# Expert stage of a hybrid S5 / attention / MoE layer: token lists from a DRAM table, padded bias rows, longer lo parts, paired PSUM banks

## Chip, cores and metric

One core of one Trainium2 chip runs the whole layer in one launch. The metric is the device time of a run in microseconds (us); lower is better.

## The reference

The layer normalises 1024 tokens of 1024 channels (with 256 context tokens beside them), mixes them by a state-space branch and a windowed attention, and then sends each token to 4 of 32 experts. The change touches only that last part:

```python
logits = (xf @ w_router + b_router)
top_v, top_i = lax.top_k(logits, 4)
gates = jax.nn.softmax(top_v, axis=-1)
...
gu = xb @ w_gate_up[e] + b_gate_up[e]
glu, lin = jnp.split(gu, 2, axis=-1)
glu = jnp.minimum(glu, 7.0)
lin = jnp.clip(lin, -7.0, 7.0)
act = glu * jax.nn.sigmoid(1.702 * glu) * (lin + 1)
return act @ w_down[e] + b_down[e]
...
y = zeros.at[row_tok].add(y_rows * row_gate[:, None])
```

All of it is float32. Each expert has a gate-and-up matrix of 1024 x 2048 and a down matrix of 1024 x 1024, 12 MB together.

## The kernel before

**Stages.** Some 1080 us of projections, state-space scan, attention and router come first; then the 32 experts run one after the other (about 1090 to 2670 us); a last stage normalises and stores. The change is in the expert stage and in the small preparations just ahead of it.

**Precision.** A float32 product is made of three TensorE products. A weight tile is split into a high part `wh`, written by ScalarE (ACT, line 1491), and a low part `wl = raw - wh`, by VectorE (DVE, line 1493). Both are computed in `Weights.prepare` for a piece of 1 MB, in two halves of 1024 columns, with a half's `wl` right behind its `wh`. Raw pieces come by 512 KB transfers on SyncE's queue, up to 8 halves ahead; `wh` and `wl` have four buffers each.

**Experts.** `ORDER` takes the experts by rank of their number of tokens, one from the top and one from the bottom in turn: 15 *wide* ones of two blocks (128 + 128 down to 128 + 32 rows) and 17 *narrow* ones of one block of 128. I call the place in that order the position, from 0; even positions up to 28 are wide. Every expert has 12 steps: 0 to 7 the up product (`up`/`act` when narrow, `up_wide`/`act_wide` when wide), 8 to 11 the down product (`down`). In each step the program emits, for TensorE (PE), ACT and DVE in an order written by hand: the part of the elementwise work that is due (`after`), the split of the weights of a later step (`prepare`), a turn of the next expert's rows in steps 1, 6, 7 and 10 (`x_parts`: four transposes on TensorE, line 1277, into a bank `tp`, a high copy on ACT, a subtraction on DVE, line 1286), and then the step's matmuls (`main`). In steps 5 and 9 of a narrow expert the activations are turned as well (`TURN`, line 1277 with `tp<-ident,t`).

**Lists.** Which tokens an expert gets is found by one-hot matrices: `places` makes `oh` (8 DVE instructions, line 1197), and `slots` multiplies `info` by it (8 matmuls of 6 columns per block, each with its weight load, line 1213, tile `sl`), sums and decodes on DVE (lines 1217 to 1226) and gives row indices `ri`, destinations `wi` and gates `gt`. This is done two positions ahead. Then GpSimd (POOL) gathers the rows (`x<-xm_d`, line 1255) and, after the expert, adds results to `acc_d` with an indirect DMA (line 1442). GpSimd executes its queue in order.

**Bias.** A wide expert adds its bias on ACT. A narrow one adds it with a matmul at line 1320: `sel` (64 rows, one of them set by `pick`) times `bgu` (64 rows), once per pair of up steps, 4 times an expert.

**PSUM.** Five banks `mm` rotate among products, two `tp` among turns, one `lg` is for `sl`.

Of the kernel before, what the change touches and what calls it, by code (L numbers as in the profile page):

```python
# [19 lines left out]
D = 1024  # L20
# [61 lines left out]
def body(tc, a, o):  # L82
# [3 lines left out]
    with es:  # L86
# [20 lines left out]
        K.tabe_d = dram.tile([64, 1], I32, name="tabe_d")  # L107
        K.cst = cst
# [973 lines left out]
def rank_consts(tc, a, K, tmp):  # L1082
    nc = tc.nc
    v = nc.vector
    late = K.late
    K.g2 = late.tile([128, D], F32, name="g2")
# [15 lines left out]
    K.pick = late.tile([64, 32], F32, name="pick")  # L1102
# [39 lines left out]
def ranks(tc, a, K):  # L1142
# [30 lines left out]
    v.tensor_copy(K.pick, K.pk.bitcast(F32))  # L1173
# [27 lines left out]
def slots(tc, K, pool, ps, o, info, blocks, steps=((0, 6),)):  # L1201
# [5 lines left out]
    p = ps.tile([128, 512], F32, tag="lg", name="sl")  # L1207
    out = [(pool.tile([128, 1], I32, tag="ri%d" % b, name="ri"), pool.tile([128, 1], I32, tag="wi%d" % b, name="wi"),
            pool.tile([128, 1], F32, tag="gt%d" % b, name="gt")) for b in range(len(blocks))]
    for c0, c1 in steps:  # L1210
# [16 lines left out]
        yield out  # L1227

# [4 lines left out]
class Expert:  # L1233
# [76 lines left out]

    def up(self, c, w):

        nc, K = self.nc, self.K
        if c % 2 == 0:
            self.gu = K.mm.tile([128, 512], F32, tag="mm", name="up")
# [16 lines left out]
    def act(self, q):  # L1332
# [3 lines left out]
        x = self.whole(self.gu, nb, ("hg", "hu")[q])[0:nb]  # L1336
        t = P.tmp.tile([128, 512], F32, tag=("sg", "um")[q], name="t")[0:nb]
# [10 lines left out]
    def up_wide(self, c, w):  # L1348
# [5 lines left out]
        self.uw = []  # L1354
        for i in range(2):
            p = K.mm.tile([128, 512], F32, tag="mm", name="uw")
# [4 lines left out]
            self.uw.append(p[:, 0:2 * n].rearrange("p (q n) -> p q n", q=2))  # L1361

    def act_wide(self, c):
# [4 lines left out]
        t = [P.tmp.tile([128, 512], F32, tag=("sg", "um")[q], name="t") for _ in range(2)]  # L1368
        x, y = [a[:, 0:n] for a in t], [a[:, 256:256 + n] for a in t]
        for i in range(2):  # L1370
            nc.scalar.activation(out=y[i], in_=self.uw[i][:, 1], func=ACTF.Identity, bias=self.bias[:, q * 8 + j0 + i:q * 8 + j0 + i + 1])  # L1371
        for i in range(2):
            v.tensor_tensor(x[i], self.uw[i][:, 0], y[i], ALU.add)
        if q == 0:
            yield
            for i in range(2):
                nc.scalar.activation(out=y[i], in_=x[i], func=ACTF.Sigmoid, scale=SWIGLU)
            yield
            for i in range(2):
                v.tensor_tensor(x[i], x[i], y[i], ALU.mult)  # L1380
            self.g = x
            return
        for i in range(2):
            v.tensor_scalar(x[i], x[i], LIMIT + 1, 1 - LIMIT, ALU.min, ALU.max)
        for i in range(2):
            v.scalar_tensor_tensor(x[i], self.g[i], TOP, x[i], ALU.min, ALU.mult)
        yield
        for i in range(2):
            nc.scalar.activation(out=self.a[:, j0 + i, 0:n], in_=x[i], func=ACTF.Copy)
        yield  # L1390
        for i in range(2):
# [30 lines left out]
    def down(self, c, k0, w):  # L1422
        if k0 == 0:
            if c == 0:
                self.y = []
            self.y.append([self.K.mm.tile([128, 512], F32, tag="mm", name="dn")[0:nb if nb > 64 else 2 * nb] for nb in self.blocks])
# [24 lines left out]
class Weights:  # L1451
# [8 lines left out]
    def add(self, eid, wide=False):  # L1460
        for m, kn, k, c in WIDE if wide else CHUNKS:
            self.todo += [(eid, m, kn // 2, k + i * kn // 2, c) for i in range(2)]

    def fetch(self):
# [5 lines left out]
        n = 1024 // kn  # L1470
# [3 lines left out]
        nc.sync.dma_start(out=r, in_=w[:, k:k + kn])  # L1474
        self.raw.append(r)

    def prepare(self):
# [6 lines left out]
        kn, n = self.raw[0].shape[1:3]  # L1484
        hi = P.ws.tile([128, 2 * kn, n], F32R, tag="wh", name="wh")
        lo = P.ws.tile([128, 2 * kn, n], F32R, tag="wl", name="wl")
        self.ready.append((hi, lo))
        for i in range(2):
# [17 lines left out]
def expert_pools(tc, a, K, es, deep):  # L1506
    P = Ctx()
    pool = lambda name, bufs=1, **k: es.enter_context(tc.tile_pool(name=name, bufs=bufs, **k))
    P.ahead = 8 if deep else 4
# [5 lines left out]
    P.tmp = pool("etmp", 2)  # L1515
# [69 lines left out]
def expert_consts(tc, a, K, late):  # L1585
    nc = tc.nc
    K.bgu = late.tile([64, 2 * D], F32R, name="bgu")
    K.full = late.tile([64, 256], F32, name="full")
    nc.gpsimd.memset(K.full, 1.0)
    nc.gpsimd.memset(K.full[:, 192:256], 0.0)  # L1590
    br = K.wp.tile([128, KT, 256], F32, tag="raw", name="br").rearrange("p k n -> p (k n)")[0:64]
    for j in range(2):
        nc.sync.dma_start(out=br[j * 32:(j + 1) * 32], in_=a["b_gate_up"])
    nc.gpsimd.tensor_scalar(br[:, D:], br[:, D:], 1.0, 1.0, ALU.add, ALU.mult)
# [6 lines left out]
def moe(tc, a, K):  # L1601
    nc = tc.nc
    es = ExitStack()
    with es:
        pool = lambda st, name, bufs=1, **k: st.enter_context(tc.tile_pool(name=name, bufs=bufs, **k))
        K.mm = pool(es, "emm", 5, space=PSUM)
        K.tp = pool(es, "etp", 2, space=PSUM)
        K.lg = pool(es, "elg", 1, space=PSUM)
        with ExitStack() as st:
# [7 lines left out]
            def expert_id(nc, K, r):  # L1617
                if r not in regs:
                    regs[r] = nc.sync.value_load((eid if P.ahead == 8 else K.eid)[0:1, r:r + 1], min_val=0, max_val=31)
                return regs[r]  # L1620

            def place(i):
                if i < len(ORDER):
                    r = ORDER[i]
                    return places(tc, K, P.li, lambda t: K.posr[:, t, r:r + 1], CAPS[r])

            def lists(i, o, *steps):
                if i < len(ORDER):
                    r = ORDER[i]
                    return slots(tc, K, P.li, K.lg, o, lambda t: K.info[:, t, r, :], BLOCKS[CAPS[r]], *steps)  # L1630
# [9 lines left out]
            P.ahead = 2  # L1640
            with tc.manual_schedule(engines={mybir.EngineType.PE, mybir.EngineType.DVE, mybir.EngineType.Activation}):
# [7 lines left out]
                P.ahead = 8  # L1649
# [8 lines left out]
            prev = None  # L1658
            with tc.manual_schedule(engines={mybir.EngineType.PE, mybir.EngineType.DVE, mybir.EngineType.Activation}):
                for i in range(len(ORDER)):  # L1660
                    xs = iter(nxt.x_parts()) if nxt else iter(())
                    for c in range(12):
# [4 lines left out]
                        weave(prev.store(1) if c == 0 and prev else None, cur.after(c), W.prepare(), x)  # L1667
# [54 lines left out]
def rest(tc, a, K):  # L1722
    nc = tc.nc
    v = nc.vector
    with ExitStack() as es:
# [4 lines left out]
        with tc.For_i(0, count, 1) as i:  # L1730
# [484 lines left out]
def host(inputs):  # L2215
# [16 lines left out]
    w["route"] = route_table()  # L2232
    w["sink"] = f("attn_sink")[0]
# [26 lines left out]
```

## Time and profile before

| what | value |
|---|---|
| median of 3 runs | 2745.44 us (2743.88 to 2748.95) |
| the profiled execution | 2748.94 us |
| its span in the profile | 2746.8 us |
| mean granted TensorE clock | 0.948 |
| PE / DVE / ACT / POOL busy, share of the span | 91% / 80% / 54% / 10% |
| moved by DMA | 662.57 MB, 241 GB/s in the mean |

The span is the time from the first instruction to the last; 2.1 us of the profiled execution lie around it. Busy shares are means over stages with different limits: in the first 1080 us several engines take turns, in the expert stage TensorE hardly stops. The chain of work that ended last holds only the closing normalisation, so it tells little of the expert stage.

### The profile page before, as it was taken

The page shows a single profiled execution, that of the slowest core. Times are in us where ns is not written, and L with a number is a line of the kernel's source. Part 1 is how long each engine was busy: PE and PEld are TensorE (multiplying, and loading weights), DVE is VectorE, ACT ScalarE, POOL GpSimd, SP SyncE. Part 2 cuts the span into 40 slices and gives each one's busy share as a digit, 9 for nine tenths or more (in the row PEclk, how much of TensorE's full clock was granted, in tenths as well). Part 3 has the DMA queues.
Part 4 walks back from the last instruction along what each step waited for, and adds up shares of the span by engine and source line. Part 5 has one row for each costly group of instructions (what it writes and reads, how often), then busy time and mean ns, then how long its engine had stood idle before and what let it go on. Part 6 is the DMA issues. An engine that isn't in the chain of part 4 may idle for free. (4 is left out here: it accounts for less than half of the span.)

```text
span 2746.8 us, 41465 instructions
## 1 busy us (share of the span) xinstructions
PE 2513.2 (91%) x14030; PEld 2113.3 (77%) x14030; DVE 2190.4 (80%) x4354; ACT 1471.6 (54%) x2394; POOL 273.7 (10%) x173
## 2 busy tenths in 40 slices
PE   6799999889989886899999999999999999999990
PEld 1598887767778775788878878888988887888770
DVE  9735797348787757787987987988989899989995
ACT  0622112657766312555665665666666666666661
POOL 3300000000000004010100100111011011101113
PEclk8799999999999876899999999999999999999995
DMA  7434623644686782797987987998998999899984
GB/s 250 163 121 145 209 92 114 181 160 156 229 303 242 278 294 97 238 287 218 299 266 239 306 271 243 308 300 252 301 305 269 288 310 306 274 298 303 311 279 146
DMA packets 400937, 662.57 MB, mean 241 GB/s; under 512 B 36976, under 2 KB 203760, under 8 KB 393616
## 3 DMA queue, kind: packets, MB, share of 16 engines
q1 hardware_dynamic: 388416, 615.83, 67.0%
q0 software_dynamic: 11872, 42.47, 6.7%
q8 instruction: 112, 1.84, 0.3%
q10 hardware_dynamic: 432, 1.57, 0.2%
q14 instruction: 105, 0.86, 0.1%
HBM read 570.63 MB, written 89.15 MB: 240 GB/s over the span
## 5 line engine op out<-in xcount | busy, mean ns | idle before, releaser
L1493 DVE TENSOR_TENSOR wl<-raw,wh 128x1024 fp32r<-128x1024 f32 x768 | 921.6, 1220 | 162.4 <-ACT wh L1491 161.4
L1491 ACT ACTIVATE wh<-raw 128x1024 fp32r<-128x1024 f32 x768 | 789.6, 1052 | 244.0 <-PE dn L1309 88.7
L1359 PE MATMUL uw<-x,wh 128*128 128x320 f32 (+5 forms) x1920 | 578.3, 365 | 0.2 <-issue 0.2
L1360 PE MATMUL uw<-x,wl 128*128 128x192 f32 (+4 forms) x1920 | 500.2, 261 | 0.0
L1359 PEld LDWEIGHTS uw<-x,wh 128*128 128x128 f32 x1920 | 363.1, 189 | 23.5 <-issue 0.3
L1360 PEld LDWEIGHTS uw<-x,wl 128*128 128x128 f32 x1920 | 368.2, 192 | 0.5
L1306 PE MATMUL dn<-wh,a 128*128 128x512 f32 (+4 forms) x752 | 298.7, 397 | 0.0
L1307 PE MATMUL dn<-wl,a 128*128 128x512 f32 (+4 forms) x752 | 293.5, 390 | 0.0
L1309 PE MATMUL dn<-wh,a 128*128 128x512 f32 (+3 forms) x608 | 238.5, 392 | 0.6 <-DVE a L1286 0.6
L1306 PE MATMUL up<-wh,x 128*128 128x512 f32 x544 | 221.8, 408 | 0.0
L1442 POOL DMA_INDIRECT acc_d<-y,wi x47 | 118.9, 2531 | 959.5 <-DVE y L1440 815.8
L1309 PE MATMUL up<-wh,x 128*128 128x512 f32 x544 | 213.0, 392 | 0.0
L1307 PE MATMUL up<-wl,x 128*128 128x512 f32 x544 | 212.3, 390 | 0.0
L1371 ACT ACTIVATE t<-uw,bias 128x160 f32<-128x160 f32 (+5 forms) x240 | 98.6, 419 | 131.8 <-PE uw L1360 130.9
L1306 PEld LDWEIGHTS dn<-wh,a 128*128 128x128 f32 (+4 forms) x752 | 135.7, 180 | 37.8 <-issue 4.1
L1307 PEld LDWEIGHTS dn<-wl,a 128*128 128x128 f32 (+4 forms) x752 | 135.8, 181 | 33.8
L1309 PEld LDWEIGHTS dn<-wh,a 128*128 128x128 f32 (+3 forms) x608 | 112.8, 186 | 28.4 <-DVE a L1286 2.7
L1306 PEld LDWEIGHTS up<-wh,x 128*128 128x128 f32 x544 | 102.3, 188 | 27.4 <-issue 8.4
L1309 PEld LDWEIGHTS up<-wh,x 128*128 128x128 f32 x544 | 102.1, 188 | 22.4
L1307 PEld LDWEIGHTS up<-wl,x 128*128 128x128 f32 x544 | 102.4, 188 | 18.8
L51 PE MATMUL mm<-whi,uh 128*128 128x256 f32 x320 | 108.4, 339 | 4.4 <-DVE r L307 4.4
L52 PE MATMUL mm<-wlo,uh 128*128 128x256 f32 x320 | 107.7, 337 | 0.0
(529 smaller groups left out, 4970.7 us busy)
## 6 DMA issues: line engine op xcount, KB each, us to landing
raw<-w_gate_up SPq DMA_DIRECT2D x512, 512.0 KB
raw<-w_down SPq DMA_DIRECT2D x256, 512.0 KB
mw<-w_mod SPq DMA_DIRECT2D x64, 256.0 KB
raw<-w_in SPq DMA_DIRECT2D x13, 1024.0 KB
whi<-wo SPq DMA_DIRECT2D x10, 1024.0 KB
wlo<-wo SPq DMA_DIRECT2D x10, 1024.0 KB
raw<-w_mod SPq DMA_DIRECT2D x8, 1024.0 KB
gate_d<-gs SPq DMA_DIRECT2D x16, 512.0 KB
```

Of the source, the lines that this page charges most:

```text
L51: nc.tensor.matmul(out, lhsT=lsel(lh, k), rhs=rsel(rh, k), start=start and k == 0, stop=False)
L52: nc.tensor.matmul(out, lhsT=lsel(lh, k), rhs=rsel(rl, k), start=False, stop=False)
L1306: nc.tensor.matmul(ps, lhsT=h, rhs=wh[:, k], start=st, stop=False)
L1307: nc.tensor.matmul(ps, lhsT=h, rhs=wl[:, k], start=False, stop=en and nb <= 64)
L1309: nc.tensor.matmul(ps, lhsT=X[:, k0 + k, lo:lo + nb], rhs=wh[:, k], start=False, stop=en)
L1359: nc.tensor.matmul(p[:, 0:2 * n], lhsT=wh[:, k, fs], rhs=self.x[:, k, 0:2 * n], start=k == 0, stop=False)
L1360: nc.tensor.matmul(p[:, 0:m], lhsT=wl[:, k, fs], rhs=self.x[:, k, 0:m], start=False, stop=k == KT - 1)
L1371: nc.scalar.activation(out=y[i], in_=self.uw[i][:, 1], func=ACTF.Identity, bias=self.bias[:, q * 8 + j0 + i:q * 8 + j0 + i + 1])
L1442: nc.gpsimd.indirect_dma_start(out=K.acc_d, out_offset=bass.IndirectOffsetOnAxis(ap=wi[0:nb], axis=0), in_=o[0:nb], in_offset=None, bounds ...
L1491: nc.scalar.activation(out=h, in_=r, func=ACTF.Copy)
L1493: nc.vector.tensor_tensor(l, r, h, ALU.subtract)
```

## The change

1. The lists of the experts at positions 6 to 31 are read from a table `list_d` in DRAM (32 x 1280 rows of 4 numbers), by small transfers on GpSimd's queue (`table`). The table is first filled with a default from an input (655 KB, on SyncE's queue), and then `spread` writes into it, two pieces of work per step in positions 0 to 2: DVE finds each token's four slots and gates, GpSimd scatters them in 32 indirect DMAs of 128 rows of 16 bytes. Positions 0 to 5 keep the one-hot way.
2. The bias matmul has 128 rows; the upper 64 rows of both operands are zeros.
3. The low part is one DVE instruction of 2048 columns, after both ACT halves of 1024; a raw tile is 1 MB, filled by two transfers.
4. A wide step has its two products in a pair of banks (`two`, two pairs), and ACT and DVE mostly work on both at once. Narrow steps have two single banks (`one`). `sl` uses a `tp` bank.
5. `rank_gates` keeps a second copy of the gates, made by ACT.

The core of the difference:

```diff
+    nc.sync.dma_start(out=K.list_d, in_=a["lists"])
...
-    p = ps.tile([128, 512], F32, tag="lg", name="sl")
+    p = ps.tile([128, 512], F32, tag="tp", name="sl")
...
+def spread(tc, K, pool):
+    nc = tc.nc
+    v = nc.vector
+    t_ = lambda n, w, d=F32: pool.tile([128] + w, d, bufs=1, name=n)
+    base, key, mx, oh = t_("lb", [32]), t_("lk", [8, 32]), t_("lx", [8, 8]), t_("lo", [4, 32])
+    idx, pay = t_("li", [8, 4], I32), t_("lp", [8, 4, 4], I32)
+    v.tensor_scalar(base, K.route[:, 0:32], float(LIST), None, ALU.mult)
+    v.memset(pay, 0)
+    yield
+    v.scalar_tensor_tensor(key, K.posr, 0.0, base.unsqueeze(1).to_broadcast([128, 8, 32]), ALU.is_gt, ALU.mult)
+    yield
+    v.tensor_tensor(key, key, K.posr, ALU.add)
+    yield
+    for t in range(8):
+        v.max(out=mx[:, t], in_=key[:, t])
+        v.tensor_scalar(pay[:, t, :, 0:2], K.route[:, 64:65].unsqueeze(2).to_broadcast([128, 4, 2]), 128.0 * t, None, ALU.add)
+        yield
+    v.tensor_scalar(idx, mx[:, :, 0:4], -1.0, None, ALU.add)
+    for t in range(8):
+        yield
+        v.tensor_tensor(oh, key[:, t].unsqueeze(1).to_broadcast([128, 4, 32]), mx[:, t, 0:4].unsqueeze(2).to_broadcast([128, 4, 32]), ALU.is_equal)
+        v.tensor_tensor(oh, oh, K.gr[:, t].unsqueeze(1).to_broadcast([128, 4, 32]), ALU.mult)
+        yield
+        v.reduce_sum(pay[:, t, :, 2].bitcast(F32), oh, axis=AX.X)
+        for j in range(4):
+            nc.gpsimd.indirect_dma_start(out=K.list_d, out_offset=bass.IndirectOffsetOnAxis(ap=idx[:, t, j:j + 1], axis=0),
+                                         in_=pay[:, t, j], in_offset=None, bounds_check=32 * LIST - 1, oob_is_err=True)
+            yield
...
-            s = P.pk.tile([64, 256], F32R, tag="pk", name="pk")
-            nc.vector.tensor_scalar(s, K.full, self.pick, None, ALU.mult)
-            self.sel = s[:, 0:128] if self.n == 128 else s[:, 128:256]
+            self.sel = P.pk.tile([128, 128], F32R, tag="pk", name="pk")
+            nc.vector.tensor_scalar(self.sel, K.full, self.pick, None, ALU.mult)
...
+    def banks(self, name):
+        return self.K.mm.tile([128, 2, 512], F32, tag="two", name=name)
...
-        for i in range(2):
-            v.tensor_tensor(x[i], self.uw[i][:, 0], y[i], ALU.add)
+            nc.scalar.activation(out=y[:, i], in_=uw[:, i, n:2 * n], func=ACTF.Identity, bias=self.bias[:, q * 8 + j0 + i:q * 8 + j0 + i + 1])
+        v.tensor_tensor(x, uw[:, :, 0:n], y, ALU.add)
...
-        for i in range(2):
-            ks = slice(i * kn, (i + 1) * kn)
-            h, l, r = (x.rearrange("p k n -> p (k n)") for x in (hi[:, ks], lo[:, ks], self.raw.pop(0)))
-            nc.scalar.activation(out=h, in_=r, func=ACTF.Copy)
-            h = h.bitcast(F32)
-            nc.vector.tensor_tensor(l, r, h, ALU.subtract)
-            yield
+        h, l, r = (x.rearrange("p k n -> p (k n)") for x in (hi, lo, raw))
+        for i in (0, 1024):
+            nc.scalar.activation(out=h[:, i:i + 1024], in_=r[:, i:i + 1024], func=ACTF.Copy)
+            if i == 0:
+                yield
+        nc.vector.tensor_tensor(l, r, h.bitcast(F32), ALU.subtract)
+        yield
...
-        K.mm = pool(es, "emm", 5, space=PSUM)
+        K.mm = pool(es, "emm", 2, space=PSUM)
         K.tp = pool(es, "etp", 2, space=PSUM)
-        K.lg = pool(es, "elg", 1, space=PSUM)
...
+            def table(r):
+                out = []
+                for b, nb in enumerate(BLOCKS[CAPS[r]]):
+                    x = P.li.tile([128, 4], I32, tag="tab%d" % b, name="tab")
+                    nc.gpsimd.dma_start(out=x[0:nb], in_=K.list_d[r * LIST + b * 128:r * LIST + b * 128 + nb])
+                    out.append((x[:, 0:1], x[:, 1:2], x[:, 2:3].bitcast(F32)))
+                yield out
...
-                        weave(prev.store(1) if c == 0 and prev else None, cur.after(c), W.prepare(), x)
+                        weave(prev.store(1) if c == 0 and prev else None, cur.after(c), W.prepare(), x, limit(to_lists, 2))
```

Two places show how instructions move. The first is GpSimd's queue at the start of the expert stage, from the last gather that is common to both (row form: line, operation, destination from sources, shape). Before:

```order
L1255 DMA x<-xm_d,ri 128x1024 x4
L1442 DMA acc_d<-y,wi 1152x1024 x2
L1255 DMA x<-xm_d,ri 128x1024
L1442 DMA acc_d<-y,wi 1152x1024
L1255 DMA x<-xm_d,ri 128x1024 x2
```

And in the change:

```order
L1294 DMA x<-xm_d,ri 128x1024 x4
L1264 DMA list_d<-lp,li 40960x4 x8
L1477 DMA acc_d<-y,wi 1152x1024
L1264 DMA list_d<-lp,li 40960x4
L1477 DMA acc_d<-y,wi 1152x1024
L1264 DMA list_d<-lp,li 40960x4 x6
L1294 DMA x<-xm_d,ri 128x1024
L1264 DMA list_d<-lp,li 40960x4 x9
L1477 DMA acc_d<-y,wi 1152x1024
L1264 DMA list_d<-lp,li 40960x4 x8
L1294 DMA x<-xm_d,ri 128x1024 x2
```

The gather of the expert at position 3 now has 15 scatters (`list_d<-lp,li`) ahead of it, that of position 4 all 32; each scatter waits for the landing of the one before it.

The second place is DVE's order in steps 1 to 5 of the narrow expert at position 29 (`x` and `a` are subtractions of a turn, `t` the activation). Before:

```order
L1493 TENSOR_TENSOR wl<-raw,wh 128x1024 x2
L1286 TENSOR_TENSOR x<-tp,x 128x4x128
L1493 TENSOR_TENSOR wl<-raw,wh 128x1024
L1341 TENSOR_TENSOR t<-up,t 128x512
L1493 TENSOR_TENSOR wl<-raw,wh 128x1024
L1197 TENSOR_SCALAR oh<-iota,posr 128x128 x8
L1493 TENSOR_TENSOR wl<-raw,wh 128x1024 x2
L1344 TENSOR_SCALAR t<-up 128x512
L1345 SCALAR_TENSOR_TENSOR t<-t 128x512
L1493 TENSOR_TENSOR wl<-raw,wh 128x1024 x2
L1217 TENSOR_REDUCE L<-sl 128x6
```

And in the change:

```order
L1530 TENSOR_TENSOR wl<-raw,wh 128x2048
L1324 TENSOR_TENSOR x<-tp,x 128x4x128
L1382 TENSOR_TENSOR t<-up,t 128x512
L1530 TENSOR_TENSOR wl<-raw,wh 128x2048 x2
L1385 TENSOR_SCALAR t<-up 128x512
L1386 SCALAR_TENSOR_TENSOR t<-t 128x512
L1530 TENSOR_TENSOR wl<-raw,wh 128x2048
L1324 TENSOR_TENSOR a<-tp,a 128x4x128
```

The one-hot instructions and the list reduction are gone, and the activation's instruction L1385 stands behind two whole low parts of 2048 columns, where before the halves left room between them.

## Rows read from the trace of the kernel before

**Rows 1.** Busy time by stretch: length, busy us (instructions) of each engine, clock, DMA share, GB/s
```profile
1150.00:2650.00 1500.00, 1494.50 (x8177) 1263.91 (x8176) 1324.29 (x2389) 963.49 (x1371) 165.31 (x89) 1.00 0.90 285
2300.00:2324.00 24.00, 23.69 (x115) 18.22 (x114) 23.28 (x33) 15.62 (x20) 3.12 (x2) 1.00 1.07 365
```

**Rows 2.** Waits between 1150 and 2650 us: total us, times, longest
```profile
ACT t L1371 <- PE uw L1360: 120.4, 93, 2.4
...
PE tp L1277 <- DVE t L1345: 4.6, 15, 0.3
...
PE dn L1309 <- DVE a L1286: 0.6, 2, 0.3
...
ACT wh L1491 <- DMA raw<-w_down: 0.4, 1, 0.4
```

**Rows 3.** PE in order of time, bias matmul: start, us, line, operation, out<-in
```profile
2104.58 0.39 PE L1307 MATMUL up<-wl,x 128*128 128x512 f32 x1
2104.81 0.39 PE L1309 MATMUL up<-wh,x 128*128 128x512 f32 x1
2105.13 0.49 PE L1320 MATMUL up<-bgu,pk 64*128 64x512 f32 x1
2105.55 0.50 PE L1306 MATMUL up<-wh,x 128*128 128x512 f32 x1
2105.88 0.39 PE L1307 MATMUL up<-wl,x 128*128 128x512 f32 x1
```

**Rows 4.** PE in order of time, steps into a turn of 32 and of 128 rows
```profile
2122.00 0.39 PE L1309 MATMUL up<-wh,x 128*128 128x512 f32 x1
2122.32 0.62 PE L1277 MATMUL tp<-ident,x 32*128 32x32 f32 x4
...
2619.65 0.39 PE L1309 MATMUL up<-wh,x 128*128 128x512 f32 x1
2619.88 0.60 PE L1277 MATMUL tp<-ident,t 128*128 128x128 f32 x4
```

**Rows 5.** PE in order of time, list matmuls in a wide expert
```profile
1869.64 1.93 PE L1213 MATMUL sl<-info,oh 128*128 128x6 bf16 x16
1871.50 0.44 PE L1359 MATMUL uw<-x,wh 128*128 128x384 f32 x1
```

**Rows 6.** PE in order of time, list matmuls and turn in a narrow expert
```profile
2114.49 0.35 PE L1213 MATMUL sl<-info,oh 128*128 128x6 bf16 x8
2115.15 0.66 PE L1277 MATMUL tp<-ident,t 128*128 128x128 f32 x4 [0.30 <-DVE t L1345]
```

**Rows 7.** DVE in order of time, the same narrow expert
```profile
2110.11 1.39 DVE L1197 TENSOR_SCALAR oh<-iota,posr 128x128 bf16<-128x128 bf16 x8
2111.41 2.35 DVE L1493 TENSOR_TENSOR wl<-raw,wh 128x1024 fp32r<-128x1024 f32 x2
...
2117.28 0.20 DVE L1217 TENSOR_REDUCE L<-sl 128x6 f32<-128x48 f32 x1
```

**Rows 8.** PE in order of time, start of the expert stage
```profile
1103.08 1.97 PE L1277 MATMUL tp<-ident,x 128*128 128x128 f32 x8 [7.60 <-DVE x L1286]
...
1105.65 0.77 PE L1359 MATMUL uw<-x,wh 128*128 128x512 f32 x1 [0.20 <-issue]
...
1120.86 1.12 PE L1277 MATMUL tp<-ident,x 128*128 128x128 f32 x4 [7.30 <-DMA x<-xm_d,ri]
```

**Rows 9.** POOL in order of time, positions 1 and 2
```profile
1198.20 3.08 POOL L1442 DMA_INDIRECT acc_d<-y,wi  x1 [7.21 <-DVE oh L1197]
...
1255.07 1.09 POOL L1255 DMA_INDIRECT x<-xm_d,ri  x1 [24.46 <-DVE L L1217]
```

**Rows 10.** PE in order of time, first turn of the rows of position 4
```profile
1295.30 0.60 PE L1277 MATMUL tp<-ident,x 128*128 128x128 f32 x4
```

**Rows 11.** All gathers between 1130 and 2650 us, on GpSimd's queue
```profile
L1255 POOL DMA_INDIRECT x<-xm_d,ri x44: 991/1078/1868, 1147.6 to 2585.4; - x44
...
DMA to landing us min/median/max: 4.0/5.9/8.2
```

More of the change, by code (lines that the diff above doesn't have):

```diff
@@ L1101, in rank_consts @@
     K.eid = late.tile([1, 32], I32, name="eid")
-    K.pick = late.tile([64, 32], F32, name="pick")
+    K.pick = late.tile([128, 32], F32, name="pick")
+    v.memset(K.pick[64:128], 0.0)
     K.cnt = late.tile([64, 32], F32, name="cnt")
@@ L1186, in rank_gates @@
     v.tensor_copy(gr, p)
+    K.gr = pool.tile([128, 8, 32], F32, bufs=1, name="gr0")
+    nc.scalar.activation(out=K.gr, in_=p, func=ACTF.Copy)
     for j in range(3):
@@ L1314, in up @@
         if c % 2 == 0:
-            self.gu = K.mm.tile([128, 512], F32, tag="mm", name="up")
+            self.gu = K.mm.tile([128, 512], F32, tag="one", name="up")
         p = self.gu
@@ L1335, in act @@
         nc, P, nb = self.nc, self.P, self.n
-        x = self.whole(self.gu, nb, ("hg", "hu")[q])[0:nb]
-        t = P.tmp.tile([128, 512], F32, tag=("sg", "um")[q], name="t")[0:nb]
+        x = self.gu[0:nb]
+        t = P.tmp.tile([128, 2, 512], F32, tag=("sg", "um")[q], name="t")[0:nb, 0]
         if q == 0:
@@ L1353, in up_wide @@
         wh, wl = w
-        self.uw = []
+        t = self.banks("uw")
         for i in range(2):
-            p = K.mm.tile([128, 512], F32, tag="mm", name="uw")
+            p = t[:, i]
             fs = slice(i * 128, (i + 1) * 128)
@@ L1425, in down @@
                 self.y = []
-            self.y.append([self.K.mm.tile([128, 512], F32, tag="mm", name="dn")[0:nb if nb > 64 else 2 * nb] for nb in self.blocks])
+            dn = self.banks("dn") if self.wide else self.K.mm.tile([128, 512], F32, tag="one", name="dn").unsqueeze(1)
+            self.y.append([dn[0:nb if nb > 64 else 2 * nb, b] for b, nb in enumerate(self.blocks)])
         for b in range(len(self.blocks)):
@@ L1508, in expert_pools @@
     pool = lambda name, bufs=1, **k: es.enter_context(tc.tile_pool(name=name, bufs=bufs, **k))
-    P.ahead = 8 if deep else 4
+    P.ahead = 4 if deep else 2
     P.raw = pool("eraw", P.ahead)
@@ L1586, in expert_consts @@
     nc = tc.nc
-    K.bgu = late.tile([64, 2 * D], F32R, name="bgu")
-    K.full = late.tile([64, 256], F32, name="full")
+    K.bgu = late.tile([128, 2 * D], F32R, name="bgu")
+    K.full = late.tile([128, 128], F32, name="full")
     nc.gpsimd.memset(K.full, 1.0)
-    nc.gpsimd.memset(K.full[:, 192:256], 0.0)
-    br = K.wp.tile([128, KT, 256], F32, tag="raw", name="br").rearrange("p k n -> p (k n)")[0:64]
+    br = K.wp.tile([128, KT, 256], F32, tag="raw", name="br").rearrange("p k n -> p (k n)")
+    nc.gpsimd.memset(br[64:128], 0.0)
     for j in range(2):
         nc.sync.dma_start(out=br[j * 32:(j + 1) * 32], in_=a["b_gate_up"])
-    nc.gpsimd.tensor_scalar(br[:, D:], br[:, D:], 1.0, 1.0, ALU.add, ALU.mult)
+    nc.gpsimd.tensor_scalar(br[0:64, D:], br[0:64, D:], 1.0, 1.0, ALU.add, ALU.mult)
     for c in range(4):
@@ L1629, in lists @@
                     r = ORDER[i]
[L1630 removed]
+                    return table(r) if i >= FIRST else slots(tc, K, P.li, K.tp, o, lambda t: K.info[:, t, r, :], BLOCKS[CAPS[r]], *steps)
             def start(i, ls):
@@ L1648, in moe @@
                 regs.clear()
-                P.ahead = 8
+                P.ahead = 4
                 for x in cur.x_parts():
@@ L2232, in host @@
     w["route"] = route_table()
+    w["lists"] = np.tile(np.stack([np.zeros(128), S + np.arange(128), np.zeros(128), np.zeros(128)], axis=1), (32 * LIST // 128, 1)).astype(np.int32)
     w["sink"] = f("attn_sink")[0]
```

66 lines of the change are left out of this document (33 added, 33 removed).

## The prediction

> **What bounds the kernel now.** I read the busy table in stretches first. In the 1500 us in which the 32 experts run, TensorE (PE) is busy 1494.5 us at a granted clock of 1.00, its 2.4 GHz level; VectorE (DVE) is busy 1324, the DMA engines 0.90 of the time [rows 1]. Then the waits of that stretch: PE has only two waits on VectorE, 4.6 and 0.6 us, while ScalarE (ACT) waits 120.4 us for PE's wide products and loses 0.4 us to a raw weight that is late [rows 2]. So PE sets the pace, and it is paced by its own list of instructions: what leaves that list counts in full, unless VectorE or a transfer becomes late in its place. VectorE is near that: in a narrow stretch it is busy 23.3 of 24 us [rows 1]. Last I read single instructions in order of time.
>
> **Bias matmuls (128 rows for 64).** Ordinary up matmuls start 0.23 us apart (2104.58, 2104.81). Around a bias matmul the starts are 2104.81, 2105.13, 2105.55, 2105.88: 1.07 us for three steps that at 0.227 (the mean over a step) would be 0.68, so 0.39 too much [rows 3]. Two things differ in it: 64 rows, and the bias operands. That the rows cost it is suggested by the turns: the step from an up matmul into a turn of 32 rows takes 0.32 as well (2122.00 to 2122.32), that into a turn of 128 rows 0.23 (2619.65 to 2619.88) [rows 4]. 68 of these matmuls run, 4 in each of 17 narrow experts: 68 x 0.39 = 26.5 us at most, 1.56 per narrow expert. Below nothing is excluded: same columns, same count. I take 26.5, with 0 as the other end.
> The Trainium skill, "TensorE: Matmul & The Clock Gate", in its section on why this matters for your kernels, says that a single matmul over 32 rows takes as long as one over 128. By that rule padding brings nothing and the total would be 26 us later. The trace speaks against it as far as it goes, by the 0.39 us; no run here yet shows a bias matmul of 128 rows.
>
> **One-hot lists (sl, oh).** From the expert at position 6 on the lists come from the table; these experts' list matmuls were made two positions ahead, so they vanish from position 4 on. In the wide positions from 4 to 26 there are 16 of them; the group that starts at 1869.64 holds PE for 1.86 us, until 1871.50 [rows 5]. Nine positions show 1.76 to 1.86 like this one; the first three (256- to 208-row experts) show 0.63, 0.57 and 0.52, the last, with 8, shows 0.21: 18.2 us, and some 0.07 each for the slower matmul behind: 19. Wide positions give 19 us; VectorE has slack there. The PSUM pairs, with one instruction on both halves for two, I cost at nothing: ACT waits 120.4 us for PE at the first of them [rows 2]; if that cover were gone, a step could lose the half that now starts early, under 1 us.
> In narrow positions eight list matmuls run from 2114.49, and the turn of the activations follows at 2115.15, of which 0.30 is a wait on VectorE. A position without lists, 2619.88, has no such wait [rows 4, 6]. At most 0.66 us is to be had 13 times, 8.5 us.
>
> **Lo parts of 2048 columns.** VectorE takes 2.35 us for two halves in a row [rows 7], so one instruction of 2048 is put at 2.3: next to nothing in busy time (bounds 2.2 to 2.44, two means of 1.22). What changes is when: it can start only once both ACT halves exist, and what stands behind it waits longer. I laid out a narrow expert by hand from these durations, with 1.39 us of one-hot and some 1.2 us of list arithmetic gone from VectorE [rows 7] and PE 1.2 us earlier at step 5. The activation is then ready 14.85 us after the expert's start and PE wants it at 14.56: a wait of 0.3 as now. At step 9 it is 28.2 against 27.85: 0.35 that is not there now. A narrow expert gives 1.56 for the bias and 0.35 for its list matmuls, less 0.35 at step 9, so near 1.6; 13 of them 21 us. The last two (no lists before either) give 1.4 each, positions 1 and 3 0.3 each, and position 1 pays 3.6 for the arithmetic of the table on a full VectorE (four of eight token tiles with four instructions each, 0.9 a tile by an estimate from 0.17 to 0.2 for the small ones [rows 7]). Narrow sum: 21 + 2.8 + 0.6 - 3.6 = 21.
> Raw weights arrive as before in two 512 KB transfers, 4 MB deep instead of 4 MB in halves, but a buffer comes free later by one half. With 0.4 us of waits for raw [rows 2] I cost that at nothing; its cover is the 3 MB ahead.
>
> **Start of the stage.** Four turns of expert 0 use two banks now: PE waits 7.60 us for VectorE's subtraction until 1103.08, and the first wide matmul is at 1105.65 [rows 8]. In the change the list tile of expert 0 keeps one of the two banks, so every turn waits for the subtraction of the turn just before, and the first subtraction stands behind a 2.3 us lo part that needs both halves. Three turns of about 1.0 + 0.7 + 0.7 us in sequence end near 1110; first wide matmul at about 1111 instead of 1105.65. Part is covered: PE waits 7.30 us for expert 1's rows until 1120.86 anyway [rows 8], but their gather follows the lists, which shift nearly as far. Cost 4.5 us (4 to 5.5).
>
> **The table on GpSimd's queue.** 32 scatters of 128 rows are put ahead of the gathers of experts 3 and 4, each waiting for the landing of the one before. Let p be one such step. Positions: the second accumulate of the first expert goes at 1198.20 and takes 3.08, the gather of expert 4 now goes at 1255.07, and PE turns its rows at 1295.30 [rows 9, 10]. In the change 6 + 9 + 8 = 23 scatters, a gather (1.1), an accumulate (2.3) and two gathers (1.1 and 1.1, then 5.9 to landing) stand between: with p = 3.75 the rows land at 1201.3 + 86.3 + 3.4 + 1.1 + 5.9 = 1298, just when PE, later by the start, is there. Beyond that each us of p costs 23 us. No row shows a small scatter. Bounds: 1.1, the instruction alone, and 5.9, a gather's median landing with 512 KB [rows 11]. Nearest is the fastest gather, 4.0 us, and its 512 KB need over 1 us at the 285 GB/s of the stretch [rows 1]; I take p = 3 to 4, cost 0 to 6, say 2.
> In the Trainium skill, "DMA: Bandwidth & Descriptors", section "Anatomy of one DMA — SWDGE (gpsimd) path", a fixed part of about 2.0 us per DMA is given, nearly all of it the write's receipt. By that, an estimate, p is near 3.1 with the issue of 1.1 and the chain costs nothing; the trace's 4.0 for a gather is in line, and no row has a scatter of 2 KB.
>
> **Sum.** -19 - 21 + 4.5 + 2 = -33.5, on the profiled execution's 2748.9: 2715. That execution lies 3.5 us above the median of the three times, 2745.4, so the forecast is **2712 us**. About 0.2%, 5.5 us, is what can be told from no change.
>
> **Rivals.**
> - *The table delays experts 3 and 4* (slower). It decides from p = 3.75, eats the whole gain at p = 5.2, and at p = 6 costs 52 us: 2762. For it: VectorE is busiest there, and gathers already take up to 8.2 us to land [rows 11]; against it: 2 KB, not 512.
> - *Beside a two-input VectorE instruction GpSimd stands still.* Its DMA instruction takes 0.99 to 1.87 us [rows 11], a spread of 0.9; if the longer lo parts add 1.2 us to each of 23 steps, p grows from 3.6 to 4.8: 24 us, 2736. The Trainium skill, "SBUF — State Buffer", section "SBUF: two separate sides", says that DVE and GpSimd share a port pair under an exclusive lock, so descriptors can wait for a whole instruction. The spread would fit it, but the median of 1.08 with VectorE at 88% speaks against waits of that size.
> - *Bias rows bring nothing*: 26 us less, 2738.
> - *Activations late*: if both turns of a narrow expert wait 0.7 us longer than I laid out, 17 x 1.4 = 24 us: 2736.
> - *DMA becomes the bound*: narrow stretches already run at a share of 1.07, 365 GB/s [rows 1]. A narrow expert shorter by 1.6 of 40 us wants 4% more; if nothing of narrow time can be gained, 21 us less: 2733. Wide stretches refill, so I doubt it.
>
> **Numbers.** Forecast 0.56 (2698 to 2724), bias nothing 0.09, late activations 0.08, DMA 0.05, lock 0.08, table delay with a loss 0.14. Range 2698 to 2746, which leaves out the last case and a little below. Faster by over 0.2% (below 2740): 0.56 + 0.08 + 0.06 + 0.04 + 0.05 = 0.79; slower (above 2751) 0.13; the same 0.08.
>
> **What would show it.** Right: bias matmuls and the one behind starting 0.23 apart; no list matmuls on PE after position 3; scatters 3 to 4 us apart on GpSimd; expert 4's rows landed before PE asks; PE waits of 0.3 us on VectorE at two turns of each narrow expert; first wide matmul 5 us later. Wrong: PE waits of many us on gathered rows around 1235 and 1300; ACT waiting for raw weights; bias starts unchanged at 0.42.

## The result, and the profile after

The changed kernel takes 2794.91 us (median of 4 runs, 2790.35 to 2799.36), the one before 2747.19 in the same comparison (4 runs): a ratio of 1.0174, 95% interval 1.0152 to 1.0195, 48 us slower. Forecast was 2712. The profiled execution is the one of 2790.35 us; its span is 2788.6, the mean granted clock 0.942.

By stretch (columns as in [rows 1]), the changed kernel:

```profile
1150.00:1250.00 100.00, 79.07 (x379) 65.51 (x378) 71.47 (x90) 49.71 (x63) 28.03 (x21) 0.91 0.78 239
1250.00:1350.00 100.00, 81.18 (x420) 68.28 (x419) 61.18 (x83) 42.52 (x58) 37.49 (x29) 0.90 0.56 171
1360.00:2650.00 1290.00, 1253.22 (x6826) 1078.47 (x6825) 1039.14 (x975) 814.30 (x1094) 195.31 (x107) 1.00 0.89 285
```

PE was busy 99.6% of the expert stage before [rows 1]. Now it is busy 79 and 81% in the first two hundred us after 1150 and 97% from 1360 on. What it waits for between 1150 and 2650 us (columns as in [rows 2]):

```profile
POOL list_d L1264 <- DMA list_d<-lp,li: 86.4, 24, 7.6
...
PE tp L1315 <- DMA x<-xm_d,ri: 34.0, 2, 17.2
...
PEld dn L1344 <- DVE t L1413: 22.9, 19, 2.0
...
PE dn L1344 <- DVE t L1413: 18.0, 13, 1.8
PE tp L1315 <- DVE t L1386: 17.6, 26, 2.0
...
PE uw L1400 <- DVE t L1413: 6.5, 19, 0.7
...
ACT wh L1527 <- DMA raw<-w_gate_up: 3.4, 6, 1.3
```

Two waits are new against [rows 2], for gathered rows (34.0 us on PE) and for VectorE's read of wide products (`t`, line 1413, at the first down step and at up steps); the turn's wait has grown from 4.6 to 17.6 us. Raw weights are not the reason: ScalarE waits 3.4 us for those of `w_gate_up` and 1.2 for those of `w_down`.

By position, with the times from the first up matmul of an expert to that of the next, the two profiled executions differ so: the routing ends 12.3 us earlier (in the profiles of e2 to e12 below, which share the change's preparations, it does not end that early, so I count it as scatter of this execution, the fastest of the four); from there to position 1 +10.8 (6.8 before the first wide matmul, 4.0 in position 0); position 1 +2.4; **positions 2 and 3 +20.3 and +19.0**; the **13 wide positions from 4 on +16.8** (forecast -19); the 13 narrow ones from 5 to 29 -13.7 (forecast -21).

**The table.** GpSimd's queue while PE, in position 2, is due to turn the rows of position 3, and then PE:

```profile
1230.80 1.37 POOL L1264 DMA_INDIRECT list_d<-lp,li  x1 [5.33 <-DMA list_d<-lp,li]
1237.59 0.98 POOL L1264 DMA_INDIRECT list_d<-lp,li  x1 [5.41 <-DMA list_d<-lp,li]
1239.97 0.98 POOL L1264 DMA_INDIRECT list_d<-lp,li  x1 [1.41 <-DMA list_d<-lp,li]
1242.42 0.98 POOL L1264 DMA_INDIRECT list_d<-lp,li  x1 [1.47 <-DMA list_d<-lp,li]
1243.70 1.06 POOL L1294 DMA_INDIRECT x<-xm_d,ri  x1 [0.30 <-issue]
```

```profile
1248.33 1.09 PE L1315 MATMUL tp<-ident,x 128*128 128x128 f32 x4 [17.21 <-DMA x<-xm_d,ri]
```

The gather of position 3's rows starts at 1243.70; PE has stood for them for 17.2 us by 1248.33. All scatters of the run (duration, time to landing):

```profile
L1264 POOL DMA_INDIRECT list_d<-lp,li x32: 977/1017/2965, 1160.8 to 1327.0; - x32
...
DMA to landing us min/median/max: 1.8/4.9/8.3
```

Of the 31 steps from one scatter to the next, 24 have nothing between them but the wait for the landing; their mean is 5.0 us. Their length goes with the traffic. All engines in two stretches of that time, by busy time:

```profile
1225.00:1237.00 12.00, 6.11 (x35) 5.02 (x33) 7.17 (x10) 4.09 (x6) 1.84 (x2) 0.94 1.10 348
1237.00:1245.00 8.00, 0.00 (x0) 0.00 (x0) 0.00 (x0) 0.00 (x0) 4.00 (x4) 0.50 0.08 23
```

At a DMA share of 1.10 the step from 1230.80 takes 6.8 us; when PE has stopped and hardly any weights move, the share is 0.08 and steps take 2.4 (1237.59, 1239.97, 1242.42).

**A wide step.** VectorE, ScalarE and PE around the first down step of position 24 (160 rows):

```profile
2392.70 0.48 DVE L1413 TENSOR_TENSOR t<-uw,t 128x320 f32<-128x320 f32 x1
...
2395.55 2.29 DVE L1530 TENSOR_TENSOR wl<-raw,wh 128x2048 fp32r<-128x2048 f32 x1 [1.49 <-ACT wh L1527]
2397.76 0.68 DVE L1324 TENSOR_TENSOR x<-tp,x 128x512 fp32r<-128x512 f32 x1
...
2398.83 0.48 DVE L1413 TENSOR_TENSOR t<-uw,t 128x320 f32<-128x320 f32 x1
```

```profile
2394.10 0.47 ACT L1425 ACTIVATE a<-t 128x320 fp32r<-128x320 f32 x1 [2.05 <-DVE t L1422]
2394.48 1.04 ACT L1527 ACTIVATE wh<-raw 128x1024 fp32r<-128x1024 f32 x1
2395.43 0.66 ACT L1412 ACTIVATE t<-uw,bias 128x160 f32<-128x160 f32 x2
2395.98 1.06 ACT L1527 ACTIVATE wh<-raw 128x1024 fp32r<-128x1024 f32 x1
```

```profile
2397.37 0.25 PE L1401 MATMUL uw<-x,wl 128*128 128x192 f32 x1
2399.37 0.78 PE L1344 MATMUL dn<-wh,a 128*128 128x512 f32 x1 [1.76 <-DVE t L1413]
2399.95 0.63 PE L1345 MATMUL dn<-wl,a 128*128 128x512 f32 x1
2400.38 0.63 PE L1347 MATMUL dn<-wh,a 128*128 128x512 f32 x1
```

ScalarE puts the two `t` of the next wide step (2395.43) between the two halves of `wh`, VectorE idles 1.49 us until the second half, then needs 2.29 for the long low part, and only after two more subtractions does it read the wide products at 2398.83. PE wants their banks for the down step and waits 1.76 us; its next matmuls start 0.43 us apart instead of 0.23: from 2399.4 to 2402.4 the granted clock is 0.50, the 1.2 GHz level. At positions 20 and 26 PE waits as long there, but the granted clock stays at 1.00.

**Bias.** Starts around a bias matmul are now 0.23 apart, as forecast:

```profile
2137.36 0.40 PE L1347 MATMUL up<-wh,x 128*128 128x512 f32 x1
2137.59 0.40 PE L1361 MATMUL up<-bgu,pk 128*128 128x512 f32 x1
2137.83 0.39 PE L1344 MATMUL up<-wh,x 128*128 128x512 f32 x1
```

### The profile page after: what moved, and what is told of

Same layout as the page of the kernel before. It is cut to its first block, busy times and chain, and to the rows that moved or that the text cites. A ratio compares the mean times of both kernels' runs of the same rounds, so it can differ in the third digit from the quotient of the medians.

```text
span 2788.6 us, 39078 instructions
## 1 busy us (share of the span) xinstructions
PE 2480.4 (89%) x13726; PEld 2099.7 (75%) x13726; DVE 2086.9 (75%) x3146; ACT 1453.6 (52%) x2275; POOL 381.4 (14%) x243
## 5 line engine op out<-in xcount | busy, mean ns | idle before, releaser
L1530 DVE TENSOR_TENSOR wl<-raw,wh 128x2048 fp32r<-128x2048 f32 x384 | 877.2, 2288 | 304.1 <-ACT wh L1527 303.3
L1477 POOL DMA_INDIRECT acc_d<-y,tab x38 | 111.5, 2933 | 547.0 <-DVE y L1475 506.5
L1412 ACT ACTIVATE t<-uw,bias 128x160 f32<-128x160 f32 (+5 forms) x240 | 88.1, 417 | 75.1 <-PE uw L1401 75.0
L1294 POOL DMA_INDIRECT x<-xm_d,tab x38 | 64.4, 1694 | 362.7 <-PE tp L1315 361.2
L1315 PE MATMUL tp<-ident,x 128*128 128x128 f32 (+5 forms) x376 | 61.2, 287 | 58.3 <-DMA x<-xm_d,ri 43.3
```

What stands on the lines that cost most here:

```text
L1294: nc.gpsimd.indirect_dma_start(out=x[0:nb], out_offset=None, in_=K.xm_d, bounds_check=S - 1, oob_is_err=True, in_offset=bass.IndirectOffse ...
L1315: nc.tensor.transpose(p[:, i * nb:(i + 1) * nb], rows(i), K.ident[0:nb, 0:nb])
L1412: nc.scalar.activation(out=y[:, i], in_=uw[:, i, n:2 * n], func=ACTF.Identity, bias=self.bias[:, q * 8 + j0 + i:q * 8 + j0 + i + 1])
L1477: nc.gpsimd.indirect_dma_start(out=K.acc_d, out_offset=bass.IndirectOffsetOnAxis(ap=wi[0:nb], axis=0), in_=o[0:nb], in_offset=None, bounds ...
L1530: nc.vector.tensor_tensor(l, r, h.bitcast(F32), ALU.subtract)
```

## The experiments

All ratios are to the kernel before, from runs on the same chip. Times of single experts come from each run's profile: up and down part together, us. In the change and in e4 the experts of 160 rows take 57.9 us where the clock falls after the wait and 56.3 where it does not, so e4's 56.3 at position 24 is no gain of e4.

| kernel | position 2 | 3 | 23 (narrow) | 24 (160 rows) | ratio (95%) |
|---|---|---|---|---|---|
| before | 68.2 | 39.2 | 39.5 | 54.2 | 1 |
| the change | 88.5 | 58.2 | 38.4 | 57.9 | 1.0174 (1.0152 to 1.0195) |
| e1 bias only | 68.2 | 39.0 | 39.0 | 54.2 | 0.9975 (0.9962 to 0.9988) |
| e2 low parts in halves | 84.0 | 49.6 | 39.2 | 52.4 | 1.0012 (1.0000 to 1.0025) |
| e3 single banks | 87.3 | 57.2 | 38.3 | 54.3 | 1.0101 (1.0080 to 1.0122) |
| e4 paced table | 69.2 | 39.6 | 38.4 | 56.3 | 1.0060 (1.0039 to 1.0080) |
| e5 low parts by kind | 85.3 | 49.9 | 39.3 | 52.4 | 1.0013 (1.0000 to 1.0026) |
| e6 = e5 + paced | 68.2 | 40.7 | 39.3 | 52.4 | 0.9923 (0.9907 to 0.9940) |
| e7 = e5, no table | 68.2 | 39.2 | 42.1 | 54.2 | 1.0104 (1.0087 to 1.0121) |
| e8 = e6 + single banks | 68.2 | 39.9 | 37.8 | 52.4 | 0.9863 (0.9847 to 0.9880) |
| e9 = e8, 64 bias rows | 68.2 | 40.1 | 38.7 | 52.4 | 0.9904 (0.9882 to 0.9926) |
| e10 = e8, list bank | 68.2 | 39.6 | 37.9 | 52.4 | 0.9862 (0.9842 to 0.9882) |
| **e11 = e8, halves** | 68.2 | 40.3 | 37.3 | 52.4 | **0.9848 (0.9829 to 0.9866)** |
| e12 = e11, 64 bias rows | 68.2 | 40.3 | 38.7 | 52.4 | 0.9913 (0.9889 to 0.9937) |

**e1, e2, e3, e4: one part each.** e1 is the kernel before with the padding alone; the others undo one part of the change:

```diff
# e2
-        nc.vector.tensor_tensor(l, r, h.bitcast(F32), ALU.subtract)
-        yield
...
+            nc.vector.tensor_tensor(l[:, s], r[:, s], h[:, s].bitcast(F32), ALU.subtract)
+            yield
# e3
-        K.mm = pool(es, "emm", 2, space=PSUM)
+        K.mm = pool(es, "emm", 6, space=PSUM)
...
-        t = self.banks("uw")
...
+            p = K.mm.tile([128, 512], F32, tag="mm", name="uw")
# e4
-FIRST = 6
+FIRST = 8
...
-        ... limit(to_lists, 2))
+        ... limit(to_lists, 1))
```

> The kernel before with the bias matmul of 128 rows and nothing else of the change. Rows theory: 68 bias matmuls save 0.39 us each, 26 us, so a ratio near 0.990 to the kernel before and starts of 0.23 us around line 1320's matmul. Rival (rows do not matter, the operands do): ratio 1.000 and starts of 0.32, 0.42 and 0.33 us as before.

Measured 0.9975, 7 us where 26 were expected. PE's starts fell to 0.23 us as in the change, so the rows do cost what was said; but the narrow expert of position 23 shrank by 0.4 us, not 1.6. Its stretch, and its turn:

```profile
2288.08:2327.11 39.03, 37.69 (x182) 30.44 (x181) 38.16 (x57) 27.91 (x33) 6.36 (x3) 1.00 1.00 317
```

```profile
2304.10 0.66 PE L1277 MATMUL tp<-ident,t 128*128 128x128 f32 x4 [1.08 <-DVE t L1345]
```

VectorE is busy 38.2 of 39.0 us there: a narrow expert with one-hot lists is bound by VectorE, and what PE saves becomes a wait of 1.08 at the turn, against 0.30 in [rows 6].

> The changed kernel with the low part in two VectorE instructions of 1024 columns, each right behind its ScalarE half; raw tiles of 1 MB, bank pairs and table stay. Theory of the long low part: PE's waits on the subtraction and addition t<-uw in wide experts (0.4 to 2.0 us each) go, wide experts from position 12 on lose 2 to 5 us each, some 30 us in all, ratio to before near 1.006. Rival (two pairs of banks are the cause): the waits stay within a third, ratio 1.013 to 1.018. Positions 2 and 3 keep their 20 us each by both.

The waits on `t` are gone and position 24 takes 52.4 us, its up part 34.0: the long low part is needed for the wide loss. Over the 13 wide positions from 4 on this run is at -20.5 us against the kernel before, where the change is at +16.8. Narrow experts got slower, though (39.2 against 38.4), and the time fell a little more than expected, since positions 2 and 3 also lost less (26 us, not 39). Why they did stays open: the scatters' steps are as long as in the change (below).

> The changed kernel with six single PSUM banks in rotation and the elementwise work of wide steps by halves as before; low parts of 2048 columns and the table stay. Theory of the bank pairs: waits of PE on t<-uw go and the ratio falls to near 1.006. Rival (the long low part): a third step of slack hides part, but ACT and DVE still go round slower than PE in 160-row experts: waits at the first down step fall by less than half, ratio 1.012 to 1.018.

1.0101, between the two. e3 also goes back to elementwise work by halves in wide steps. With six banks the up part of position 24 has no wait (34.0 us), but its down product waits 1.70 us for the activations instead (line 1432): the long low part is late for PE either way, 2.0 us in all here, and the pairs make it 5.5 (57.9 against 52.4, 1.6 of it the lower clock). Over the 13 wide positions e3 is at -7.6 us: single banks alone take back about two thirds of the loss, short low parts alone all of it. The loss takes both the long low part and the pair.

> The changed kernel with the table written at one piece of work per step instead of two, so that it is done in position 4, and used from position 8 on instead of 6; everything else stays. Queue theory: each gather has about 4 scatters ahead of it instead of 15 and 17; positions 2 and 3 lose nothing (within 3 us of before) and the whole gains 35 to 40 us less 1.3 us for two more one-hot lists: ratio near 1.004. Rival (the table's arithmetic on VectorE delays the positions): the same work only spread, positions 1 to 4 stay together some 40 us longer, ratio unchanged at 1.017.

The queue theory held: positions 2 and 3 are back to within 1 us, and 31 us are gained. VectorE does the same arithmetic as in the change, only spread, so the amount of it wasn't the cause, and PE's wait of 34.0 us on gathered rows is gone.

The lengths of the scatters' steps also show how much VectorE's long instructions held GpSimd. In e2, where no low part takes over 1.23 us,

```profile
L1264 POOL DMA_INDIRECT list_d<-lp,li x32: 980/1006/2002, 1157.9 to 1320.8; - x32
...
DMA to landing us min/median/max: 1.9/5.1/8.7
```

the 24 steps with nothing else between have a mean of 5.06 us against 5.02, and of that the issue 1.19 against 1.42. So 0.23 us may be that, not the 1.2 of the rival; the rest is the landing. In the runs with a paced table, where the traffic does not pause, the means are 5.7 (e4) to 6.2 us (e8).

**e5 to e8: parts together.** In e5 `prepare` takes `not cur.wide` and makes long low parts only in narrow steps. e6 paces the table as in e4; e7 leaves out table and `spread` (`FIRST = 32`); e8 adds the single banks of e3.

> The changed kernel with the low part in two halves in the steps of wide experts and in one instruction of 2048 columns in the steps of narrow ones; table unpaced, bank pairs as in the change. Theory (a wide step needs the short low part, a narrow one is bound by VectorE and needs the long one's 1.9 us): 160-row experts up in 34.0 us as in the run with halves everywhere, narrow ones up in 25.8 and down in 12.5 as in the change; positions 2 and 3 still lose 26 to 39 us. Ratio to before 0.998 to 1.005. Rival (the loss in narrow steps with halves came from raw weights arriving late, not from VectorE): narrow experts take 39.2 us here too, since wide ones leave no more lead than there, ratio near 1.001 to 1.008.

Position 24 as expected, but narrow experts 39.3, as in e2. That is the rival's number, but not for its reason: from 1360 us on ScalarE waits 6.6 us for raw weights here, 41.7 in e2. Neither theory had the cause; e6 and e8 below show it.

> The same with the table written one piece per step and used from position 8 on. If the two causes (scatters ahead of gathers; long low parts in wide steps) are separate and all there is, their gains add: the change's 1.0174 less 0.0114 (paced) less about 0.0125 (wide low parts) gives 0.9935, and 0.990 to 0.996 is in reach: faster than both kernels. If the lead of the raw weights runs out instead, 1.000.

The two causes add: 0.9923, faster than both kernels, 2728 us. In narrow experts PE still waits at the turn, and ScalarE has a wait that [rows 2] do not have:

```profile
PE tp L1315 <- DVE t L1386: 29.9, 31, 2.4
...
ACT hg L1369 <- DVE y L1475: 32.4, 18, 2.0
```

> The same low parts, bias rows and bank pairs, but no table: all experts keep the one-hot lists and no scatter runs. It tells what the table itself is worth. Theory: list matmuls cost 18 us in wide and the one-hot's VectorE work 2.6 us in each of 13 narrow experts, of which the long low part gives 1.9 back: ratio 0.993 to 0.997, some 5 to 15 us slower than with the paced table. Rival (one-hot lists cost nothing beside other work): at or under the paced table's time, which still pays 3 to 5 us for its arithmetic at the start.

Beside long low parts in narrow steps the table is worth far more than the 5 to 15 us expected: 48 us against e6 (2775.9 and 2727.9). With one-hot instructions ahead of the activation, the turn of position 23 waits 2.79 us and the expert takes 42.1, where the kernel before, with one-hot lists and halves, takes 39.5. So the 48 us are not the table's worth by itself. Nearer to that are e1 and e11 below, both with halves, single banks and padding, without and with the table: 0.9975 and 0.9848, some 35 us (they differ in the size of raw tiles and the list's bank as well).

> The paced kernel of this call with six single PSUM banks and elementwise work by halves in wide steps. Theory: with short low parts the pairs cost PE nothing, so the same time within 3 us, at most 3 us more where VectorE's double instructions fill. Rival (the pairs still hold PE): 5 to 20 us less.

The rival's number holds: 18 us less by the medians (2710.09 and 2727.91), 15 between the two profiled executions, of which 13.6 in the narrow experts from position 13 on. Wide experts take the same 52.4 us in both, so there the pairs do cost nothing beside short low parts, as the theory said. ScalarE at the end of position 22, and PE's turn in position 23, in e6:

```profile
2266.98 1.06 ACT L1528 ACTIVATE wh<-raw 128x1024 fp32r<-128x1024 f32 x1 [2.63 <-issue]
2270.05 0.59 ACT L1369 ACTIVATE hg<-dn 32x512 f32<-32x512 f32 x1 [2.01 <-DVE y L1475]
2270.55 2.08 ACT L1528 ACTIVATE wh<-raw 128x1024 fp32r<-128x1024 f32 x2
```

```profile
2287.89 0.66 PE L1315 MATMUL tp<-ident,t 128*128 128x128 f32 x4 [1.60 <-DVE t L1386]
```

and in e8:

```profile
2261.24 1.06 ACT L1531 ACTIVATE wh<-raw 128x1024 fp32r<-128x1024 f32 x1 [2.63 <-issue]
2262.33 0.59 ACT L1366 ACTIVATE hg<-dn 32x512 f32<-32x512 f32 x1
2262.83 1.04 ACT L1531 ACTIVATE wh<-raw 128x1024 fp32r<-128x1024 f32 x1
```

```profile
2280.74 0.66 PE L1315 MATMUL tp<-ident,t 128*128 128x128 f32 x4 [0.19 <-DVE t L1383]
```

`hg` is ScalarE's copy of the second block's down result, out of PSUM. With a bank pair it waits for VectorE's `y`, which reads the first block in the other bank of the pair; with single banks it starts as soon as ScalarE is free. The `wh` behind it, the low parts and the next activation are all later, and the turn waits 1.60 us against 0.19. In the change itself this wait was small (8.5 us in 13 times), and its narrow experts take the same with pairs and without (38.4 and 38.3 in e3); it counts once wide steps run at PE's pace.

**e9 to e12: what is left.**

> The fastest kernel so far (low parts by the kind of expert, paced table, single banks) with the bias matmul back to 64 rows. Theory: alone the padding gave only 7 us because narrow experts were bound by VectorE; here VectorE is free, PE waits just 0.19 and 0.17 us at the two turns, so the padding is worth 17 x (1.56 - up to 0.36) = 20 to 26 us: ratio to before 0.994 to 0.996 against 0.986. Rival (the padding is worth 7 us here too): 0.989.

Between the two: 0.0041, 11 us. The narrow expert gives up 0.9 us of the 1.56.

> The same fastest kernel with five single banks and a bank of its own for the list tile, as the kernel before has it. Theory of the start: the first four turns again use two banks, the first wide matmul comes 5 us earlier after the routing is done, ratio lower by 0.0015 to 0.002 (3 to 5 us), with no new waits on five banks. Rival (the start is covered by the gather of the second expert): within 1 us of the kernel with six banks.

Equal within the interval (2710.41 and 2710.09). In the profile the first wide matmul comes 26.9 us after the expert indices are ready, against 30.3, and 28.4 to 30.4 in the profiles of e2 to e9, e11 and e12, which share that bank: it costs some 1.5 to 3.5 us there, and the times of runs don't resolve it.

> The fastest kernel (paced table, six single banks) with the low part in halves of 1024 in all steps, narrow ones too. VectorE theory: a long low part saves VectorE 1.9 us in a narrow expert, and narrow experts stand close to VectorE's time, so here they take 38.4 to 39.2 us instead of 37.8, ratio 0.989 to 0.992 against 0.986. Rival (the loss of the runs with halves and bank pairs was only ScalarE's copy held up by the pair): narrow experts as in the fastest kernel, ratio 0.986.

The rival again: once single banks let ScalarE go on, halves cost nothing in narrow experts, and by the two profiles they gain (37.3 against 37.8 us at position 23). 2706.96 us is the fastest median of the study, but e8's interval overlaps. Its positions 23 and 24:

```profile
2259.63:2296.96 37.33, 37.33 (x174) 30.26 (x173) 36.18 (x42) 27.92 (x33) 9.30 (x5) 1.00 0.98 315
2296.96:2349.33 52.37, 52.37 (x346) 47.31 (x345) 44.30 (x88) 34.72 (x60) 3.18 (x3) 1.00 0.91 304
```

PE is busy 37.33 of 37.33 and 52.37 of 52.37 us. ScalarE now waits 49 us for raw weights from 1360 us on, without holding PE at these two positions.

> The last kernel (halves everywhere, single banks, paced table) with the bias matmul of 64 rows. There PE never waited more than 0.4 us in a narrow expert from position 19 on, so the padding should show nearly its full instruction price: 17 x 1.3 to 1.56 = 22 to 26 us, ratio 0.9928 to 0.9943. Rival (as in the kernel with long low parts, 11 us): ratio 0.989.

0.9913: the padding is worth 0.0065 here, 18 us; 1.4 us per narrow expert, less in positions 1 to 5, where one-hot lists and the table's arithmetic still take VectorE's time (no run tests that by itself).

## Why the prediction was wrong

The sum was -33.5 us. The best recombination, e11, gives -42 (0.9848) with the padded bias rows, the table (paced) and neither long low parts nor pairs, so the gains were there. Against the sum, the change's profile loses 37 us more at positions 2 and 3, 36 in the wide positions, 6 from the routing to position 1 and 7 in the narrow ones, and its routing ends 12 us earlier. The first two are costs put at nothing or next to it. 2795 us is above every rival too (the highest was 2762): the rivals weighed one cause at a time, and two came together.

1. **"I take p = 3 to 4, cost 0 to 6, say 2."** The term was mis-sized: p, the step from one scatter to the next, was 5.0, and 5.7 to 6.2 in the paced runs, where the traffic doesn't pause. The formula behind it, 23 us for each us above 3.75, gives 29 us; the loss was 39 at positions 2 and 3, and pacing gave 31 back. The first rival had the mechanism and the place. I took the fastest gather (4.0) as nearest because a scatter moves 2 KB; but a small transfer's landing went with what else was in flight (2.4 us a step at a share of 0.08, 6.8 at 1.10), and [rows 11]'s median of 5.9, under that same traffic, was the nearer row. The Trainium skill, "DMA: Bandwidth & Descriptors", section "Anatomy of one DMA — SWDGE (gpsimd) path", with its fixed part of 2.0 us, led to an estimate of 3.1; the 2.4 us of the quiet queue lie under that, the loaded queue's 5 to 6 us far above.
2. **"VectorE has slack there. The PSUM pairs ... I cost at nothing."** This step failed: slack in busy time is not slack in latency. I laid out a narrow expert by hand and no wide one. There the low part's new place behind both halves of `wh`, with ScalarE's `t` between them, comes so late that VectorE reads the wide products after PE wants their banks. e2 shows that halves remove the loss, e3 that single banks alone remove two thirds of it, and e6 and e8 that pairs beside short low parts cost wide steps nothing. Wide positions gave +17 where -19 was forecast: 36 us, the largest error beside the table.
3. **The pair as one buffer.** ScalarE's wait for VectorE's read of the other bank was in no rival. It is no part of the change's loss (narrow experts take the same in e3), but it costs 14 to 18 us between e6 and e8, in narrow experts, which I had treated as untouched by the pairs.
4. **"What leaves that list counts in full, unless VectorE or a transfer becomes late in its place."** In narrow experts the exception was the rule: VectorE's 23.3 of 24 us was in [rows 1], yet I booked 26.5 us for the padding. Alone it gave 7, at best 18, and the change's narrow positions gave 13.7 us where 21 was forecast. The price of the rows was right: 0.39 us each. The Trainium skill, "TensorE: Matmul & The Clock Gate", in its section on why this matters for your kernels, has a matmul over 32 rows take as long as one over 128; this case measures otherwise for a 64-row one between matmuls of 128 rows (0.32, 0.42, 0.33 in [rows 3] and in e12, against 0.23 in e1). No run has a bias matmul of 32 rows.
5. **Right:** the wide positions' 1.85 us for the list matmuls (54.2 to 52.4, in e2, e5, e6 and e8 to e12); raw weights and DMA not the bound. The narrow schedule of -1.6 with waits of 0.3 and 0.35 comes out in e8 (-1.63, waits of 0.19 and 0.17), but not in the change (1.05 a position), and e9 gives the padding only 0.9 of it: the number agrees partly by luck. The start was right in kind: 4.5 us forecast, 6.8 in the change, 3.5 to 5.5 in the other runs with a shared bank. Expert indices are ready on VectorE in the kernel before at

```profile
1080.75 0.18 DVE L1170 TENSOR_SCALAR eid<-er 1x32 int32<-1x32 f32 x1 [0.48 <-PE er L1166]
```

24.9 us ahead of its first wide matmul [rows 8], and in the changed one at

```profile
1068.45 0.18 DVE L1175 TENSOR_SCALAR eid<-er 1x32 int32<-1x32 f32 x1 [1.03 <-PE er L1171]
```

31.7 us ahead of it, with each turn behind the subtraction of the one before:

```profile
1093.74 1.12 PE L1315 MATMUL tp<-ident,x 128*128 128x128 f32 x4 [10.02 <-DVE x L1324]
1096.27 1.12 PE L1315 MATMUL tp<-ident,x 128*128 128x128 f32 x4 [1.41 <-DVE x L1324]
1098.81 1.12 PE L1315 MATMUL tp<-ident,x 128*128 128x128 f32 x4 [1.41 <-DVE x L1324]
...
1100.19 0.77 PE L1400 MATMUL uw<-x,wh 128*128 128x512 f32 x1
```

The lock rival ("Beside a two-input VectorE instruction GpSimd stands still") adds at most 0.23 us a step in the mean, not 1.2. The Trainium skill's "SBUF — State Buffer", section "SBUF: two separate sides", describes an exclusive lock on the port pair that the two engines share. The traces neither show nor exclude it: the longest issue of a scatter is 2.97 us in the change and 2.00 in e2, but the mean hardly moves.

## What to carry to other kernels

An engine busy 80 or 90% of a stage has time to spare, but not at any moment: where two engines hand pieces to each other in order, lay out one step of each kind of work before merging small instructions into long ones. A chain of small transfers that wait for each other cost its landing time under the traffic of that very stage here, so spread it over the steps before its result is due rather than queueing it ahead of a gather. Sharing one buffer between two readers on different engines can cost a wait even where neither writes.

## What was not expected of the hardware

A 2 KB scatter's step from issue to the next issue was 2.4 us at a DMA share of 0.08 and 6.8 at 1.10; the means are 5.0 us in the change and up to 6.2 in the paced runs. After an idle of 1.76 us the granted clock was 0.50 for 3 us and PE's matmuls of 512 columns started 0.43 us apart at position 24, but not at position 20 after the same idle. VectorE's subtraction of 2048 columns takes 2.29 us, two of 1024 in a row 2.35: nothing is won by length.
